# Split activations and split weights laid out in changing orders in SBUF

## The chip, the cores and the metric

The kernel runs on one core of a Trainium2 chip. The metric is the device time of one execution in microseconds (us). TensorE (PE) multiplies: a weight load (LDWEIGHTS, PEld in the profile) brings 128 columns of a stationary operand into the array, and a matmul streams a moving operand past it and adds into a bank of PSUM. VectorE (DVE), ScalarE (ACT) and GpSimd (POOL) work element by element; SyncE (SP) issues most of the DMAs from HBM. SBUF holds 128 partitions; what is called the layout here is the order of elements within a partition.

## The reference

Two layers over 256 tokens of 2048 channels, all in float32: a state-space mixer (S5) with a gated output, then attention over a sliding window of 128; each is followed by a SwiGLU feed-forward of width 5632. Before each part and at the end stands a norm.

```python
def reference(x, ...):
    h = x
    for i in range(DEPTH):
        hn = rmsnorm(h, norm_mix[i])
        if i % N_MIXERS == 0:
            mix = s5_mixer(hn, ...)            # out = gl[..., :dm] * sigmoid(gl[..., dm:]), gl = gelu(y) @ w_glu
        else:
            mix = sliding_window_attention(hn, ...)   # hn @ w_qkv + b_qkv, softmax with sinks, o @ w_o
        h = h + mix
        hn = rmsnorm(h, norm_ffn[i])
        h = h + swiglu(hn, ...)                # (silu(x @ w_gate) * (x @ w_up)) @ w_down
    return rmsnorm(h, norm_final)
```

## The kernel before

**Products in three passes.** The matmuls read float32 in a form called float32r here, with less precision than float32. So every weight and every activation is split into a high part (the value rounded to float32r) and a low part (what is left), and each product is three matmuls: high x high, high x low and low x high. These are lines 734, 735 and 736 in `products`. The activations are the stationary operand (128 channels on partitions, 128 tokens as columns), the weights the moving one (128 channels, 512 columns), and the sum of 128 tokens x 512 outputs is one PSUM bank, `acc`.

**Weights.** `Weights` cuts all weight matrices into 332 pieces of 512 x 512 in the order in which they are used: 32 for the gate of S5, 88 + 44 for the first feed-forward, 20 for queries, keys and values, 16 for the attention's output, 88 + 44 for the second. A piece is loaded by one DMA of SP (`load`, L106) into a tile `raw` as [128 partitions, 4 blocks `a`, 512]. `split` then has ACT write the high part (L120) and DVE the low part (L121) into a tile `w` of [128, 2 parts, 4 blocks, 512], 16 KB a partition. There are three places for `w`, used in turns (`place`): two in the pool `wq`, one in the pool `wp`; the piece with a number that is a multiple of three goes to `wp`. `next` hands out piece i, has pieces up to i + 2 split and up to i + 4 loaded.

**Activations.** Four kinds of tiles hold split activations, each of [128 channels, 2 parts, 4 blocks, 256 tokens] and 8 KB a partition: `gt` (the gelu outputs of S5), `hT` (the hidden values of the feed-forward) and `oT` (the attention's outputs), all from `turned_tile` in the pool `pp`; and `xT` (the normed rows, turned), from `normed_tile` in the pool `wp`. PE turns blocks of 128 x 128 into PSUM, ACT writes the high part from there, and DVE the low part: L777 and L778 for `xT`, L857 and L858 for `hT`, L687 and L688 for `gt`, L1008 and L1009 for `oT`.

**Order.** `linear` makes 128 tokens x 512 outputs twice: for each piece it goes over four blocks and two halves of the tokens, so a piece is 4 x 2 x 3 = 24 matmuls (`piece`). Between pieces it takes small jobs from two lists, `left` and `slots`: turning the activations that an earlier product made, loading `h`, or a part of the attention. A framework puts the instructions of each engine in order by its own scheduling, sets the semaphores, and hands out the places of the tiles (`bufs` is the number of places of a tag); `pin` and `keep_in_program_order` hold an instruction in its written place.

**Before the products.** `s5` computes S5 itself: DVE steps through the states (L500, L503, L505), and PE does small products in plain float32. In it lie two lines that the prediction reads: L259 in `lay`, which turns 128 x 128 blocks of `Bn` (in which the columns taken lie 16 elements apart) and of `Cn` (in which they lie next to each other); and L594 in `lags`, where the moving operand is `k[:, :, g2]`, runs of 16 elements with the next 16 left out. ACT and DVE write (L453, L451) and read (L655) the state tiles `V` with a step of 64 elements between neighbours; L600 writes runs of 16 elements.

**Pools in SBUF.** In the order in which they are opened: `cp` (`ident`, 128 elements; `gcol`, 48; `ylast`, 512), `pp` (four tiles of 8 KB and two `raw` of 8 KB), `wq` (two `w`), and after S5 `wp` (`h`, two tiles of 8 KB; `ssq`, two of 8 elements; one `w`; `junk` and `act`; four `xT`; small ones).

Of the kernel before, what the change touches and what calls it, by code (L numbers as in the profile page):

```python
# [17 lines left out]
P = 128  # L18
D = 2048
# [27 lines left out]
def bc(ap, axis, n):  # L47
    """`ap` with a repeated axis of n put in."""
    v = ap.unsqueeze(axis)
    shape = list(v.shape)  # L50
    shape[axis] = n
    return v.to_broadcast(shape)
# [3 lines left out]
def kernel(  # L56
# [25 lines left out]
    # parts of activations, channels on partitions: [channel, high/low, 128 channels, token]  # L82
    def turned_tile(name):
        return pp.tile([P, 2, 4, T], F32R, tag="b8", name=nm(name))

    def normed_tile(name):
        return wp.tile([P, 2, 4, T], F32R, tag="xt", name=nm(name), bufs=4)

# [1 line left out]
    class Weights:  # L90
# [18 lines left out]
        def place(self, i):  # L109
            """in turns, but for the first the third place isn't there yet"""  # L110
            pool, n = (wp, 1) if i % 3 == 0 and i > 0 else (wq, 2)
            return pool.tile([P, 2, 4, 512], F32R, tag="w", name=nm("w"), bufs=n)

        def split(self, upto, keep=lambda ins: ins):
            while len(self.hl) < min(upto, len(self.src)):
                i = len(self.hl)
                self.load(i + 1)
                w = self.place(i)
                hi, lo = w[:, 0], w[:, 1]
                keep(S.activation(hi, self.raw[i], AF.Copy))  # L120
                keep(V.tensor_tensor(lo, self.raw[i], hi.bitcast(F32), op=ALU.subtract))  # L121
                self.hl.append((hi, lo))
# [40 lines left out]
    # the last heads come while the first two chunks of the outputs have what the others give  # L163
# [12 lines left out]
    # work that an earlier product left for the tensor engine, done between a later one's pieces  # L176
    left = []
    # the same, a list for each of the next pieces
    slots = []

# [1 line left out]
    def s5():  # L182
        st = ExitStack()
        with st:
# [8 lines left out]
            def pin(ins):  # L193
                """in this place among its engine's work"""
# [8 lines left out]
            # the states; until then, room for what does not stay  # L203
# [4 lines left out]
            # loads  # L208
# [34 lines left out]
            # masks: row (j, g2, c) belongs to g2 = 0 / 1 ; sign of the re / im half  # L243
# [11 lines left out]
            def lay(nat):  # L255
                """banks of [(re/im, state), channel, group]"""
# [5 lines left out]
            def laid(pts, name, sign):  # L262
                """[(re/im, state), group, channel], times a sign per partition"""
# [5 lines left out]
            # the norm of x: rows' sums of squares  # L269
# [11 lines left out]
            # the norm's weights go into B (and D)  # L281
# [5 lines left out]
            # the other norms' weights, channels on partitions  # L287
# [4 lines left out]
            # parameters, [group, state]  # L292
# [42 lines left out]
            # powers of lambda: [group, power - 1, re/im, state]  # L335
# [5 lines left out]
            def cmul(o, a, b, n):  # L341
                """o = a * b, complex, [G, n, 2, NS]; b has one power"""
# [11 lines left out]
            # q = (lambda - 1) / a ; XQ[j] = lambda^(3-j) q  # L354
# [19 lines left out]
            # the same with the state (twice) on partitions: [(2, state), power, re/im, group]  # L374
# [21 lines left out]
            # tokens: U[(j, g2, c), pair, g2' (other group's rows zero), chunk]; a quarter of the pairs  # L396
            # is eight of each half of the channels
# [24 lines left out]
            def at(pair):  # L422
                """quarter and place in it"""
# [5 lines left out]
            # X[j] = lambda^(3-j) q B ; what each chunk adds to the states  # L429
            X = []  # L430

            def turned_x(q, b):
# [3 lines left out]
                xt = lp.tile([P, 4, P], F32, tag="xt", name=nm("xt"), bufs=5)  # L436
# [18 lines left out]
            def split_groups(ap, t):  # L455
                """the quarter's groups, of an AP with groups second"""
# [30 lines left out]
            # states at the chunks' ends, for half of the quarters; what a chunk adds is there already  # L487
            reached = [0, 0]

            def step(hf, parts=1):  # L490
                """in as many parts as it takes to hide an operation's latency"""
# [19 lines left out]
            # lambda^4 in [(g2, state), product, re/im, quarter, half, pair]  # L511
# [45 lines left out]
            # D of a chunk's channels, on the diagonal: [(lag 0, g2, c), pair, c']  # L557
# [16 lines left out]
            # K[(lag, g2, c), pair, c'], lag 3 - j, and  # L574
            # M[(j, g2, c), pair, j', c'] = K of lag j' - j
# [5 lines left out]
            def kernels(t):  # L581
# [5 lines left out]
                k = lp.tile([P, 16, 2, GC], F32, tag="xt", name=nm("k"), bufs=5)  # L587
# [15 lines left out]
            # what a chunk's own tokens give its outputs  # L603
# [22 lines left out]
            # T[(re/im, state), group, j', c'] = what a chunk's first state gives its outputs  # L626
# [12 lines left out]
            # the states laid out as each chunk's first state  # L639
# [28 lines left out]
            # the states' room goes to the first weights  # L668
# [4 lines left out]
            # outputs, gelu, channels onto partitions  # L673
# [42 lines left out]
    def rms_scale(pool, ssq, shape, keep=lambda ins: ins, between=lambda: None):  # L716
        """1 / sqrt(ssq / D + eps)"""
# [14 lines left out]
    def products(acc, xq, w, a, t, first, last):  # L732
        x_ = xq[:, :, a, t * P : (t + 1) * P]
        PE.matmul(acc, x_[:, 0], w[0][:, a], start=first, stop=False)  # L734
# [3 lines left out]
    def piece(acc, xq, first, last):  # L738
        """the next piece of the weights with 512 channels"""
# [359 lines left out]
```

## Time and profile before

| | |
|---|---|
| median of the runs | 2145.8 us (2 runs, 2145.72 to 2145.88) |
| span of the profiled execution | 2144.7 us |
| PE busy in it | 2044.8 us |
| DVE, ACT, POOL busy | 1177.0, 907.1, 99.8 us |
| matmuls L734 + L735 + L736 | 3 x (1568 xT + 704 hT + 256 gt + 128 oT) = 7968 |
| read from HBM | 356.91 MB, 167 GB/s over the span |

The profile is one execution, recorded by the hardware. PE's busy time counts matmuls that overlap (a matmul with 512 columns lasts some 390 ns from its first read to its last write, and the next one begins before it has ended), so what a matmul costs is the distance from its start to the next start. A row of the timeline reads: start in us, duration in us, engine, line, operation, tiles written <- tiles read, and in brackets how long the engine had stood idle and what released it. A row of groups ends with the busy time of all, the mean ns of one, and the idle time before them with what ended it. A row on one line's instructions gives minimum / median / maximum of the duration in ns, and the first and the last start. In the windows, the first number is the length of the window; the busy times of PE, PEld, DVE, ACT and POOL follow, each with its count, then the granted clock, the DMA share and GB/s.

### The profile page before, as it was taken

The page shows a single profiled execution, that of the slowest core. Times are in us where ns is not written, and L with a number is a line of the kernel's source. Part 1 is how long each engine was busy: PE and PEld are TensorE (multiplying, and loading weights), DVE is VectorE, ACT ScalarE, POOL GpSimd, SP SyncE. Part 2 cuts the span into 40 slices and gives each one's busy share as a digit, 9 for nine tenths or more (in the row PEclk, how much of TensorE's full clock was granted, in tenths as well). Part 3 has the DMA queues.
Part 4 walks back from the last instruction along what each step waited for, and adds up shares of the span by engine and source line. Part 5 has one row for each costly group of instructions (what it writes and reads, how often), then busy time and mean ns, then how long its engine had stood idle before and what let it go on. Part 6 is the DMA issues. An engine that isn't in the chain of part 4 may idle for free.

```text
span 2144.7 us, 23467 instructions
## 1 busy us (share of the span) xinstructions
PE 2044.8 (95%) x9724; PEld 1674.3 (78%) x9724; DVE 1177.0 (55%) x1432; ACT 907.1 (42%) x957; POOL 99.8 (5%) x73
## 2 busy tenths in 40 slices
PE   5854999999999999999999999999999999999998
PEld 4754888888888888888888777888888888888886
DVE  8997554544444454445455776544444445444445
ACT  4737444433333333333344554443333333333333
POOL 6450100000000000000000000000000000000000
PEclk8767999999999999999999999999999999999999
DMA  4000666565555555565555433555555555655554
GB/s 120 1 21 21 226 196 193 181 194 178 190 186 193 180 193 192 180 194 180 196 177 185 143 118 119 177 184 189 178 195 189 184 190 184 196 182 191 187 187 156
DMA packets 182731, 360.53 MB, mean 168 GB/s; under 512 B 10592, under 2 KB 10656, under 8 KB 182240
## 3 DMA queue, kind: packets, MB, share of 16 engines
q1 hardware_dynamic: 181376, 355.54, 51.0%
q10 hardware_dynamic: 816, 2.16, 0.3%
q0 software_dynamic: 432, 1.33, 0.3%
q8 instruction: 76, 1.25, 0.2%
q14 instruction: 31, 0.25, 0.0%
HBM read 356.91 MB, written 2.10 MB: 167 GB/s over the span
## 4 chain that ended last, share of the span: by engine, by line
PE 88%; DVE 9%; ACT 1%; DMA 1%; issue 1%; DVEq 0%; ACTq 0%
PE acc L734 28%; PE acc L736 28%; PE acc L735 28%; DVE sc L500 2%; DVE V L503 1%; DVE V L505 1%; PE tr L855 1%; DVE X L469 1%; DVE w L121 1%; PE py L698 1%; PE tr L774 0%; DMA raw<-in_s_w_glu_dram 0%; PE po L1002 0%; ACT w L120 0%; PE tr L991 0%
## 5 line engine op out<-in xcount | busy, mean ns | idle before, releaser
L121 DVE TENSOR_TENSOR w<-raw,w 128x2048 fp32r<-128x2048 f32 x332 | 761.0, 2292 | 859.4 <-ACT w L120 859.4
L120 ACT ACTIVATE w<-raw 128x2048 fp32r<-128x2048 f32 x332 | 636.2, 1916 | 987.9 <-PE acc L736 843.9
L734 PE MATMUL acc<-w,xT 128*128 128x512 f32 x1568 | 618.7, 395 | 0.0
L735 PE MATMUL acc<-w,xT 128*128 128x512 f32 x1568 | 617.0, 393 | 0.0
L736 PE MATMUL acc<-w,xT 128*128 128x512 f32 x1568 | 617.0, 393 | 0.0
L736 PEld LDWEIGHTS acc<-w,xT 128*128 128x128 f32 x1568 | 294.0, 187 | 69.5 <-issue 1.0
L734 PEld LDWEIGHTS acc<-w,xT 128*128 128x128 f32 x1568 | 294.0, 188 | 68.9 <-issue 1.3
L735 PEld LDWEIGHTS acc<-w,xT 128*128 128x128 f32 x1568 | 294.0, 188 | 67.8 <-issue 0.5
L734 PE MATMUL acc<-w,hT 128*128 128x512 f32 x704 | 277.3, 394 | 0.0
L736 PE MATMUL acc<-w,hT 128*128 128x512 f32 x704 | 274.8, 391 | 0.0
L735 PE MATMUL acc<-w,hT 128*128 128x512 f32 x704 | 274.1, 390 | 0.0
L736 PEld LDWEIGHTS acc<-w,hT 128*128 128x128 f32 x704 | 132.2, 188 | 29.4
L734 PEld LDWEIGHTS acc<-w,hT 128*128 128x128 f32 x704 | 132.3, 188 | 28.2 <-ACT hT L857 1.2
L735 PEld LDWEIGHTS acc<-w,hT 128*128 128x128 f32 x704 | 132.3, 188 | 28.1
L735 PE MATMUL acc<-w,gt 128*128 128x512 f32 x256 | 99.9, 390 | 0.9 <-DVE w L121 0.9
L734 PE MATMUL acc<-w,gt 128*128 128x512 f32 x256 | 100.7, 394 | 0.0
L736 PE MATMUL acc<-w,gt 128*128 128x512 f32 x256 | 100.1, 391 | 0.0
L698 PE MATMUL py<-T,S 128*64 128x64 f32 x256 | 16.2, 241 | 51.5 <-DVE V L505 51.5
L882 DVE TENSOR_TENSOR h<-h,acc 128x512 f32<-128x512 f32 x64 | 43.6, 687 | 26.5 <-PE acc L736 26.5
L735 PEld LDWEIGHTS acc<-w,gt 128*128 128x128 f32 x256 | 48.1, 188 | 11.7 <-DVE w L121 1.5
L868 ACT ACTIVATE act<-acc,ry 128x512 f32<-128x512 f32 x44 | 30.2, 687 | 62.3 <-PE acc L736 62.1
L736 PEld LDWEIGHTS acc<-w,gt 128*128 128x128 f32 x256 | 48.1, 188 | 10.7
(241 smaller groups left out, 1471.0 us busy)
## 6 DMA issues: line engine op xcount, KB each, us to landing
raw<-in_ffn_w_gate_dram SPq DMA_DIRECT2D x88, 1024.0 KB, 5.2
raw<-in_ffn_w_up_dram SPq DMA_DIRECT2D x88, 1024.0 KB, 5.2
raw<-in_ffn_w_down_dram SPq DMA_DIRECT2D x88, 1024.0 KB, 5.1
raw<-in_s_w_glu_dram SPq DMA_DIRECT2D x32, 1024.0 KB, 5.3
raw<-in_attn_w_qkv_dram SPq DMA_DIRECT2D x20, 1024.0 KB, 5.1
raw<-in_attn_w_o_dram SPq DMA_DIRECT2D x16, 1024.0 KB, 5.0
xk<-in_x_dram SPq DMA_DIRECT2D x8, 256.0 KB, 7.2
h<-in_x_dram SPq DMA_DIRECT2D x2, 1024.0 KB, 7.6
```

Source lines behind the costliest of these rows:

```text
L120: keep(S.activation(hi, self.raw[i], AF.Copy))
L121: keep(V.tensor_tensor(lo, self.raw[i], hi.bitcast(F32), op=ALU.subtract))
L469: ins = eng.tensor_tensor(o[:, :, j].rearrange("p (h a) (g c) -> p h a g c", g=2, h=2), bc(split_groups(XQT[:, j, ri], t).rearrange("p h ( ...
L500: V.tensor_tensor(t_, ws[..., part], bc(Vt[hf][:, k - 1, :, part], 1, 2), op=ALU.mult)
L503: V.tensor_tensor(v, v, t_[:, 0], op=ALU.add)
L505: V.tensor_tensor(v, v, t_[:, 1, ::-1], op=ALU.add)
L698: PE.matmul(py[m][h * NK : (h + 1) * NK, i, g2], St[t][:, a, g2], Tt[q][:, 2 * pq + g2].rearrange("p a b -> p (a b)"), start=False, stop=i ...
L734: PE.matmul(acc, x_[:, 0], w[0][:, a], start=first, stop=False)
L735: PE.matmul(acc, x_[:, 0], w[1][:, a], start=False, stop=False)
L736: PE.matmul(acc, x_[:, 1], w[0][:, a], start=False, stop=last)
L868: S.activation(s, pg[t], AF.Silu, scale=r[0][:, t : t + 1])
L882: V.tensor_tensor(hc, hc, acc[t], op=ALU.add)
```

## The change

No operation is added or removed. Four things change.

- **Order of split activations.** A tile is now 2048 elements a partition, seen in one of four orders in turns: parts, blocks, tokens ("r a n", as before); blocks, tokens, parts ("a n r", neighbouring tokens 2 elements apart); parts, tokens, blocks ("r n a", 4 apart); tokens, blocks, parts ("n a r", 8 apart). The four `xT` tiles of a norm take the four orders one each; the tiles of `turned_tile` go through them backwards.
- **Order of split weights.** A piece is now four blocks, and in each block the two parts lie in turns of e elements: 16, 32, 64, 128, or whole rows of 512. In one piece of six (e = -512) the rows are read backwards by PE, and the product writes the bank of sums backwards.
- **Where tiles begin.** `cp` has a pad of 48 elements more, and `ssq` is 32 elements instead of 8.
- **Fewer places.** `xt` (and `k`) of S5 5 to 4, `junk` 2 to 1, `bias` 2 to 1, `pT` 3 to 2.

Comments and docstrings go as well.

```diff
+    ORDERS = ("r a n", "a n r", "r n a", "n a r")
+    TOGETHER = (512, -512, 16, 32, 64, 128)
+    turn = [0, 0]
+
+    def part(t, kind):
+        return t.rearrange(f"p ({ORDERS[kind]}) -> p r a n", r=2, a=4)
+
     def turned_tile(name):
-        return pp.tile([P, 2, 4, T], F32R, tag="b8", name=nm(name))
+        turn[0] += 1
+        return part(pp.tile([P, 8 * T], F32R, tag="b8", name=nm(name)), turn[0] * 3 % 4)
 
     def normed_tile(name):
-        return wp.tile([P, 2, 4, T], F32R, tag="xt", name=nm(name), bufs=4)
+        turn[1] += 1
+        t = wp.tile([P, 8 * T], F32R, tag="xt", name=nm(name), bufs=4)
+        return part(t, (turn[1] - 1) % 4)
...
             pool, n = (wp, 1) if i % 3 == 0 and i > 0 else (wq, 2)
-            return pool.tile([P, 2, 4, 512], F32R, tag="w", name=nm("w"), bufs=n)
+            return pool.tile([P, 4096], F32R, tag="w", name=nm("w"), bufs=n)
 
         def split(self, upto, keep=lambda ins: ins):
             while len(self.hl) < min(upto, len(self.src)):
                 i = len(self.hl)
                 self.load(i + 1)
                 w = self.place(i)
+                e = TOGETHER[(i // 3 + 2 * i) % 6]
+                n = abs(e)
+                w = w.rearrange("p (a g r e) -> p r a g e", a=4, r=2, e=n)
+                raw = self.raw[i].rearrange("p a (g e) -> p a g e", e=n)
                 hi, lo = w[:, 0], w[:, 1]
-                keep(S.activation(hi, self.raw[i], AF.Copy))
-                keep(V.tensor_tensor(lo, self.raw[i], hi.bitcast(F32), op=ALU.subtract))
-                self.hl.append((hi, lo))
+                keep(S.activation(hi, raw, AF.Copy))
+                keep(V.tensor_tensor(lo, raw, hi.bitcast(F32), op=ALU.subtract))
+                if e < 0:
+                    hi, lo = hi[..., ::-1], lo[..., ::-1]
+                self.hl.append((hi, lo, e < 0))
...
+    cp.tile([P, 48], F32, name="pad")
...
-                xt = lp.tile([P, 4, P], F32, tag="xt", name=nm("xt"), bufs=5)
+                xt = lp.tile([P, 4, P], F32, tag="xt", name=nm("xt"), bufs=4)
...
     def products(acc, xq, w, a, t, first, last):
         x_ = xq[:, :, a, t * P : (t + 1) * P]
+        if w[2]:
+            acc = acc[:, ::-1]
         PE.matmul(acc, x_[:, 0], w[0][:, a], start=first, stop=False)
...
-            self.ssq = wp.tile([P, 2, NCH], F32, tag="ssq", name=nm("ssq"), bufs=2)
+            ssq = wp.tile([P, 32], F32, tag="ssq", name=nm("ssq"), bufs=2)
+            self.ssq = ssq[:, : 2 * NCH].rearrange("p (t n) -> p t n", t=2)
...
-            junk = wp.tile([P, 512], F32, tag="junk", name=nm("junk"), bufs=2)
+            junk = wp.tile([P, 512], F32, tag="junk", name=nm("junk"), bufs=1)
...
-                b = ap.tile([P, 512], F32, tag="bias", name=nm("bias"), bufs=2)
+                b = ap.tile([P, 512], F32, tag="bias", name=nm("bias"), bufs=1)
...
-                        pT = ap.tile([P, 3, P], F32, tag="pT", name=nm("pT"), bufs=3)
+                        pT = ap.tile([P, 3, P], F32, tag="pT", name=nm("pT"), bufs=2)
```

More of the change, by code (lines that the diff above doesn't have):

```diff
@@ L586, in kernels @@
                               start=True, stop=True)
[L587 removed]
+                k = lp.tile([P, 16, 2, GC], F32, tag="xt", name=nm("k"), bufs=4)
                 pin(S.copy(k, pk))
```

## The prediction

> **What bounds the kernel.** I read the page first: the span, the busy shares, the slices, the clock and the chain.
>
> ```profile
> span 2144.7 us, 23467 instructions
> PE 2044.8 (95%) x9724; PEld 1674.3 (78%) x9724; DVE 1177.0 (55%) x1432; ACT 907.1 (42%) x957; POOL 99.8 (5%) x73
> ...
> PE   5854999999999999999999999999999999999998
> ...
> PEclk8767999999999999999999999999999999999999
> ...
> PE 88%; DVE 9%; ACT 1%; DMA 1%; issue 1%; DVEq 0%; ACTq 0%
> PE acc L734 28%; PE acc L736 28%; PE acc L735 28%; DVE sc L500 2%; DVE V L503 1%; DVE V L505 1%; PE tr L855 1%; DVE X L469 1%; DVE w L121 1%; PE py L698 1%; PE tr L774 0%; DMA raw<-in_s_w_glu_dram 0%; PE po L1002 0%; ACT w L120 0%; PE tr L991 0%
> ```
>
> The chain is 88% TensorE, 83% of it in the three matmuls L734 to L736. From the fifth slice on PE is at nine tenths and the granted clock too. Next come the windows, cut at the first long product; columns are PE, PEld, DVE, ACT, POOL busy, then the clock.
>
> ```profile
> 0.00:238.00 238.00, 150.97 (x1149) 134.23 (x1149) 205.07 (x593) 134.28 (x231) 98.15 (x70) 0.74 0.21 61
> 238.00:2136.00 1898.00, 1893.70 (x8575) 1540.03 (x8575) 968.84 (x831) 771.14 (x723) 1.62 (x3) 1.00 0.56 181
> ```
>
> In the last 1898 us PE is busy for 1893.70 at clock 1.00, so no wait is left there to remove. That stretch is 332 pieces of weights with 24 matmuls each, 7968 in all, and the time between two matmul starts (the pitch) is the kernel. In the first 238 us DVE is busy for 205 and the clock is 0.74: another regime, which the change hardly touches.
>
> The pitch is read best from ACT, which begins a split 0.2 us after a piece has freed its place; the distance of two starts is one piece. The first four lines are pieces with xT as stationary operand, the last four with hT.
>
> ```profile
> 956.78 1.92 ACT L120 ACTIVATE w<-raw 128x2048 fp32r<-128x2048 f32 x1 [2.97 <-PE acc L736]
> 962.38 1.91 ACT L120 ACTIVATE w<-raw 128x2048 fp32r<-128x2048 f32 x1 [3.68 <-PE acc L736]
> 967.98 1.92 ACT L120 ACTIVATE w<-raw 128x2048 fp32r<-128x2048 f32 x1 [3.69 <-PE acc L736]
> 973.44 1.93 ACT L120 ACTIVATE w<-raw 128x2048 fp32r<-128x2048 f32 x1 [3.54 <-PE acc L736]
> ...
> 1001.66 1.92 ACT L120 ACTIVATE w<-raw 128x2048 fp32r<-128x2048 f32 x1 [3.52 <-PE acc L736]
> 1007.17 1.93 ACT L120 ACTIVATE w<-raw 128x2048 fp32r<-128x2048 f32 x1 [3.59 <-DVE h L882]
> 1012.66 1.92 ACT L120 ACTIVATE w<-raw 128x2048 fp32r<-128x2048 f32 x1 [3.56 <-PE acc L736]
> 1018.10 1.92 ACT L120 ACTIVATE w<-raw 128x2048 fp32r<-128x2048 f32 x1 [3.52 <-PE acc L736]
> ```
>
> With xT, two pieces take 5.60 us (233.3 ns a matmul) and the third 5.46 (227.5). With hT the three take 5.51, 5.49 and 5.44. The slow ones are those whose operands begin 64 bytes apart, modulo 128. Added up in the order of use, cp holds 512 + 192 + 2048 = 2752 bytes, 64 more than a multiple of 128, so hT, gt, oT and two of the three places of w begin at 64; in wp two ssq of 32 bytes bring w and xT to 0. (That cp itself begins at a multiple of 128 is assumed.) xT against w in wq: 64 apart, 5.60; against w in wp: 0 apart, 5.46; hT against w in wp: 64 apart, 5.51, else 5.49 and 5.44. So the load and the stream do meet in SBUF, and it costs 0.14 us a piece, 5.8 ns a matmul.
>
> ```profile
> L734 PE MATMUL acc<-w,xT 128*128 128x512 f32 x1568 | 618.7, 395 | 0.0
> ...
> L734 PEld LDWEIGHTS acc<-w,xT 128*128 128x128 f32 x1568 | 294.0, 188 | 68.9 <-issue 1.3
> ```
>
> The load of the next stationary operand takes 188 ns beside a matmul and fits inside the pitch: 39 to 45 ns are spare. The 1568 matmuls a line make 196 pieces with xT; 136 are left for the others. Mean pitch: (196 x (2 x 5.60 + 5.46) / 3 + 136 x 5.48) / 332 = 5.52 us a piece, 230 ns.
>
> **The change, part by part.** No matmul, split, load or DMA is added or taken away. What moves is how operands lie.
>
> *Stationary operands.* xT, hT, gt and oT cycle through four orders with tokens 1, 2, 4 and 8 elements apart (4 to 32 bytes), a quarter each. Only one stationary operand of before is not contiguous: Bn at L259, 16 elements (64 bytes) apart; Cn on the same line is contiguous.
>
> ```profile
> L259 PEld LDWEIGHTS ps<-ident,Bn x16: 187/226/227, 11.5 to 14.6; 128*128 128x128 f32 x16
> L259 PE MATMUL ps<-ident,Bn x16: 417/418/480, 11.5 to 14.8; 128*128 128x128 f32 x16
> L259 PEld LDWEIGHTS ps<-ident,Cn x16: 185/231/232, 24.9 to 28.0; 128*128 128x128 f32 x16
> L259 PE MATMUL ps<-ident,Cn x16: 420/421/477, 24.9 to 28.2; 128*128 128x128 f32 x16
> ```
>
> First of its row the load takes 187 ns (strided) against 185, in the queue 226 against 231, and sixteen take 3.1 us both times. Those loads ran at half clock or unrecorded clock and with ordinary float32, so this is no full proof, but they fetch one element from each of 128 places in no more time. I take 0 for the load. From above: ACT reads V 256 bytes apart in 1068 ns where a contiguous copy of the same size takes 587 (rows below), 1.82 times; a load 1.82 times 188 is 342 ns, which no longer fits in 230. From below: 0, since a load gets no shorter than contiguous. I choose by the first row because it is the same engine and port.
>
> *Moving operands.* w has high and low parts in turns of 16, 32, 64 or 128 elements, or in whole rows of 512, or rows read backwards with the sum written backwards (a sixth each). Of the turns the trace has the smallest: L594 streams k in runs of 16 with 16 left out, L596 is contiguous and follows it directly.
>
> ```profile
> 116.36 2.06 PE L594 MATMUL ko<-k,own 128*128 128x256 f32 x4
> 118.34 1.22 PE L596 MATMUL ko<-dd,ident 32*128 32x128 f32 x4
> 119.49 2.08 PE L594 MATMUL ko<-k,own 128*128 128x256 f32 x4
> ```
>
> Four matmuls of 256 columns take 118.34 - 116.36 = 1.98 us, four of 128 contiguous ones 1.15: per column 1.93 against 2.25 ns, so runs cost nothing; I take 0. Nothing in the trace runs backwards. Bounds: 0, since each line and bank is touched as often as forwards, and a pitch twice as long. I take 0, nearer to the runs.
>
> *Where tiles begin.* A pad of 192 bytes and ssq of 128 instead of 32 bring all these operands to 0 modulo 128. If every piece went at the aligned rate, 131 pieces with xT would gain 0.14 us (18.3) and 45 with hT, gt or oT 0.07 (3.2): 21.5 us. But parts in turns begin at 64 again and spread tokens meet other lines than before. Bounds: 0 and -21.5; I take half, -11.
>
> *The splits and the writes of the spread tiles.*
>
> ```profile
> L121 DVE TENSOR_TENSOR w<-raw,w 128x2048 fp32r<-128x2048 f32 x332 | 761.0, 2292 | 859.4 <-ACT w L120 859.4
> L120 ACT ACTIVATE w<-raw 128x2048 fp32r<-128x2048 f32 x332 | 636.2, 1916 | 987.9 <-PE acc L736 843.9 <-DVE h L882 89.7 <-DMA raw<-in_s_w_glu_dram 19.5
> ...
> L858 DVE TENSOR_TENSOR hT<-tr,hT 128x512 fp32r<-128x512 f32 x44 | 28.2, 682 | 0.0
> ...
> L453 ACT COPY V<-pv 64x256 f32<-64x256 f32 x44 | 26.2, 599 | 4.0 <-PE pv L443 3.4
> ...
> L857 ACT CAST hT<-tr 128x512 fp32r<-128x512 f32 x44 | 23.2, 579 | 0.0
> ...
> L655 ACT COPY S<-V 64x512 f32<-64x512 f32 x16 | 17.1, 1068 | 29.0 <-DVE V L505 28.9
> ...
> L451 DVE COPY V<-pv 64x256 f32<-64x256 f32 x20 | 12.0, 598 | 3.2 <-ACT V L453 2.7
> ...
> L600 ACT COPY M<-ko 32x256 f32<-32x256 f32 x40 | 14.6, 364 | 7.6 <-PE ko L596 7.1
> ...
> L1009 DVE TENSOR_TENSOR oT<-po,oT 128x256 fp32r<-128x256 f32 x16 | 6.6, 415 | 12.2 <-ACT oT L1008 12.2
> ...
> L1008 ACT CAST oT<-po 128x256 fp32r<-128x256 f32 x16 | 5.9, 368 | 22.8 <-PE po L1004 22.8
> ...
> L588 ACT COPY k<-pk 128x512 f32<-128x512 f32 x4 | 2.3, 587 | 12.2 <-PE pk L585 12.2
> ```
>
> The split writes runs of 64 bytes or more. L600 writes just that (64-byte runs, 364 ns against 368 for a contiguous 256), so L120 and L121 stay; even at twice 1.92 and 2.29 us they would end within two pieces of 5.5. Tokens 16 or 32 bytes apart, half of the tiles, may cost what L453 does (256 bytes apart): 599 - 368 = 231 ns for 256 elements on ACT, and 598 - 415 = 183 on DVE. For hT that is 0.46 us on 579 and 0.37 on 682. This hides behind pieces of 5.5 us, except where the next matmul asks for hT at once:
>
> ```profile
> PEld acc L734 <- ACT hT L857: 1.2, 4, 0.4
> ```
>
> Four such waits, each up to two writes of 0.46 longer: at most 3.7, half of it taken: +2. The same at the end of S5, where 16 casts to gt (half of them spread, 0.23 each) stand shortly before the first product: 0 to 3.7, +2 taken.
>
> *Fewer buffers.* xt 5 to 4, pT 3 to 2, junk 2 to 1: a reader of the place handed out next stands earlier on PE (or the writer is ACT itself, in order), so the writer waits for nothing new; 0. Without that cover pT would wait for a PE matmul four times in a group, under 1 us each. bias 2 to 1:
>
> ```profile
> L1026 ACT ACTIVATE bias<-bias 128x512 f32<-128x512 f32 x4 | 2.5, 632 | 17.4 <-DMA bias<-in_attn_b_qkv_dram 17.4
> ```
>
> ACT stands in this multiplication until POOL's DMA lands, and the next split stands behind it on ACT and PE behind that. Now the DMA is issued one chunk later, after the DVE reads of the chunk before; with four pieces (22 us) until q reads it, and a wait of 17.4 / 4 = 4.4 us each as now, it comes at another moment and takes no more time; 0. If ACT stood there 11 us, a piece would come late.
>
> *Sum.* 2144.7 (this execution's span) - 11 + 2 + 2 = 2137.7. The runs' median of 2145.8 is 1.1 above the span: **2139 us**, -0.3%.
>
> **Rivals.**
>
> *Loads collide in proportion to their lines* (slower, the other side). Being 64 bytes apart costs 5.8 ns for a load of contiguous tokens. If every load paid that by the places it touches, 1, 2, 4 and 4 times as many: 5.8, 11.7, 23.3, 23.3, a mean of 16 ns on the aligned 227.5. 7968 x 16 = 128, less the 21.5: +106, **2252 us**. For it: the 5.60 and 5.46 above. Against it: Bn. It decides from a mean pitch of 235 on (2% is 43 us or 5.4 ns).
>
> *The load outlasts the matmul.* Half of the matmuls at 342 ns: 3984 x 112 = 446, **2592 us**. For it: the rows of ACT and DVE (L655, L453, L451). Against it: L259, and that 39 ns are spare. The Trainium skill (Advanced Engine Details and Errata, SBUF Cachelines) says that full speed needs at least two hits on a 16-byte line; by that rule 4-byte tokens 16 and 32 bytes apart are slow and 8 apart are not. Here ACT's L453 agrees with it and TensorE's L259 does not.
>
> *Backwards costs double.* 55 pieces, 1328 matmuls, 230 ns more each: +305, **2451 us**. Nothing in the trace speaks for or against it. The Trainium skill (PSUM — Partial Sum Buffer, Specifications) says that any non-contiguous pattern in PSUM slows matmuls; whether a step of -1 counts as one it does not say, and no run here shows it yet.
>
> *Turns take the two streams apart.* If parts in turns kept load and stream from meeting at all, another step of 5.8 ns under 227.5 could go: pitch 221.7, 8.3 under the mean, 7968 x 8.3 = 66: **2080 us**. For it: that where operands lie matters at all. Against it: no row goes under 5.44 us a piece.
>
> **How the numbers follow.** "No change", everything between 2103 and 2189, has 0.58: the engine that decides shows no cost in the two rows nearest to the change. Its own range is 2117 to 2160 (the full alignment gain, or none with the writes at their ends and a few us of meeting). Proportional collision has 0.18, the long load 0.08, backwards 0.06, together 0.32 slower by over 2% (about what a measurement of this kernel can tell from no change). Faster by over 2% has 0.10. The range 2070 to 2290 takes in no change, the proportional case (2252, or 2274 without the alignment gain) and most of the faster one: 0.58 + 0.18 + 0.06 = 0.82.
>
> **What would show it.** Mean LDWEIGHTS of L734 to L736 still 188 ns, and pieces of equal length whatever the order of the tokens, prove the first step; pieces of two lengths in step with xT's four orders prove a collision or a long load, and the load's mean tells which (188 or about 340). Backwards shows as every sixth piece long, in MATMUL durations beyond 395. Alignment shows as 5.46 where 5.60 stood. Spread writes show in L778 and L858 and in waits of PE for hT. Wrong it is if one of the six ways of w or of the four of the tokens alone is slow: the mean of any one counts by a sixth or a quarter, and a quarter at +24 ns is already 2%.

## The result, and the profile after

| | before | after |
|---|---|---|
| median of the runs, us | 2145.8 | 2205.93 (2 runs, 2205.89 to 2205.97) |
| ratio, 95% interval | | 1.0279 [1.0259, 1.0298] |
| span of the profiled execution, us | 2144.7 | 2204.2 |

The changed kernel is slower, by 60 us or 2.8%. First the page of the changed kernel: the span, the busy times, and groups of the first of the three product lines (L756 to L758 now) and of the writes to `hT` (L880 and L881). A group ends with busy time and mean ns of one, then the idle time before them.

```profile
span 2204.2 us, 23485 instructions
...
PE 2104.8 (95%) x9724; PEld 1907.6 (87%) x9724; DVE 1197.7 (54%) x1432; ACT 928.6 (42%) x957; POOL 98.2 (4%) x73
...
L756 PE MATMUL acc<-w,xT 128*128 128x512 f32 x1568 | 630.8, 402 | 0.0
...
L756 PEld LDWEIGHTS acc<-w,xT 128*128 128x128 f32 x1568 | 400.0, 255 | 34.0 <-issue 1.3
...
L756 PEld LDWEIGHTS acc<-w,hT 128*128 128x128 f32 x704 | 183.4, 261 | 14.9 <-ACT hT L880 1.4
...
L881 DVE TENSOR_TENSOR hT<-tr,hT 128x512 fp32r<-128x512 f32 x44 | 38.5, 918 | 0.0
...
L880 ACT CAST hT<-tr 128x512 fp32r<-128x512 f32 x44 | 36.1, 904 | 0.0
```

The number of matmuls and loads is the same, but the mean load went from 188 to 255 ns and PEld's busy time from 1674 to 1908 us. PE still waits for nothing: the idle time before L756 with `xT` stays at 0.0. The windows, cut at the same first edge as before, show where the time came in (length; then busy times of PE, PEld, DVE, ACT, POOL; granted clock, DMA share, GB/s).

```profile
0.00:238.00 238.00, 149.80 (x1140) 135.85 (x1141) 206.59 (x593) 135.28 (x230) 96.00 (x69) 0.74 0.20 60
238.00:2196.00 1958.00, 1955.04 (x8585) 1771.74 (x8584) 988.29 (x832) 791.64 (x724) 2.17 (x4) 1.00 0.54 176
```

The stretch of the products was 1898 us long and is 1958 at the same clock of 1.00: 60 us, all of the difference, or 7.5 ns on each of 7968 matmuls. So the pitch grew. Which pieces grew is read, as before, from the starts of ACT's split: the distance of two rows is one piece.

```profile
986.32 1.92 ACT L136 ACTIVATE w<-raw 128x2048 fp32r<-128x2048 f32 x1 [3.67 <-PE acc L758]
991.97 1.91 ACT L136 ACTIVATE w<-raw 128x2048 fp32r<-128x2048 f32 x1 [3.73 <-PE acc L758]
...
1044.38 1.92 ACT L136 ACTIVATE w<-raw 128x2048 fp32r<-128x2048 f32 x1 [3.79 <-PE acc L758]
1050.24 1.91 ACT L136 ACTIVATE w<-raw 128x2048 fp32r<-128x2048 f32 x1 [3.95 <-PE acc L758]
1055.94 1.92 ACT L136 ACTIVATE w<-raw 128x2048 fp32r<-128x2048 f32 x1 [3.79 <-PE acc L758]
1061.42 1.92 ACT L136 ACTIVATE w<-raw 128x2048 fp32r<-128x2048 f32 x1 [3.55 <-PE acc L758]
1067.34 1.92 ACT L136 ACTIVATE w<-raw 128x2048 fp32r<-128x2048 f32 x1 [4.01 <-PE acc L758]
1073.04 1.92 ACT L136 ACTIVATE w<-raw 128x2048 fp32r<-128x2048 f32 x1 [3.78 <-PE acc L758]
1078.64 1.91 ACT L136 ACTIVATE w<-raw 128x2048 fp32r<-128x2048 f32 x1 [3.68 <-PE acc L758]
```

In order of time: tokens 4 apart with whole rows 5.65 us; then, from 1044.38 on, 8 apart with whole rows 5.86, 2 apart with turns of 16 5.70, 1 apart with turns of 64 5.48, 8 apart backwards 5.92, 1 apart with turns of 32 5.70, 2 apart with turns of 128 5.60. The lengths follow both orders. The mean pitch of each pair, from the starts of L756 to L758 over the whole trace without the gaps between pieces, in ns:

| tokens apart | 512 | 512 backwards | 16 | 32 | 64 | 128 | mean load |
|---|---|---|---|---|---|---|---|
| 1 | 228.0 | 233.4 | 241.8 | 237.3 | 227.9 | 228.1 | 188 |
| 2 | 233.7 | 234.0 | 237.9 | 237.9 | 233.0 | 233.1 | 195 |
| 4 | 235.1 | 233.3 | 239.9 | 241.1 | 235.0 | 235.2 | 310 |
| 8 | 244.5 | 246.9 | 238.7 | 243.4 | 244.3 | 244.4 | 327 |

The mean of these is 237, of before 230.2. The load can be seen piece by piece: the rows of L756 within a single piece each, tokens 1, 2, 4 and 8 apart (minimum, median, maximum of the duration in ns; first and last start).

```profile
L756 PEld LDWEIGHTS acc<-w,xT x8: 187/188/194, 1090.5 to 1095.3; 128*128 128x128 f32 x8
...
L756 PEld LDWEIGHTS acc<-w,xT x8: 193/193/308, 981.0 to 985.9; 128*128 128x128 f32 x8
...
L756 PEld LDWEIGHTS acc<-w,xT x9: 308/310/320, 985.9 to 991.5; 128*128 128x128 f32 x9
...
L756 PEld LDWEIGHTS acc<-w,xT x9: 192/330/333, 1084.0 to 1089.8; 128*128 128x128 f32 x9
```

8 bytes between tokens leave the load almost as it was, 16 and 32 bytes make it 1.65 and 1.76 times as long. (The odd 308 and 192 belong to a neighbouring piece.)

### The profile page after: what moved, and what is told of

It is laid out like the page before. It is cut to its first block, busy times and chain, and to the rows that moved or that the text cites. A ratio compares the mean times of both kernels' runs of the same rounds, so it can differ in the third digit from the quotient of the medians.

```text
span 2204.2 us, 23485 instructions
## 1 busy us (share of the span) xinstructions
PE 2104.8 (95%) x9724; PEld 1907.6 (87%) x9724; DVE 1197.7 (54%) x1432; ACT 928.6 (42%) x957; POOL 98.2 (4%) x73
## 4 chain that ended last, share of the span: by engine, by line
PE 87%; DVE 9%; ACT 2%; issue 1%; DMA 0%; DVEq 0%; SPq 0%; ACTq 0%; POOLq 0%
PE acc L756 28%; PE acc L758 28%; PE acc L757 28%; DVE sc L520 2%; DVE V L525 1%; DVE V L523 1%; PE tr L878 1%; DVE X L489 1%; ACT sc L998 1%; DVE w L137 1%; PE tr L796 0%; PE po L1025 0%; PE tr L1014 0%; PE py L718 0%; DVE sc L986 0%
## 5 line engine op out<-in xcount | busy, mean ns | idle before, releaser
L756 PE MATMUL acc<-w,xT 128*128 128x512 f32 x1568 | 630.8, 402 | 0.0
L758 PE MATMUL acc<-w,xT 128*128 128x512 f32 x1568 | 628.4, 401 | 0.0
L757 PE MATMUL acc<-w,xT 128*128 128x512 f32 x1568 | 627.4, 400 | 0.0
L756 PEld LDWEIGHTS acc<-w,xT 128*128 128x128 f32 x1568 | 400.0, 255 | 34.0 <-issue 1.3
L757 PEld LDWEIGHTS acc<-w,xT 128*128 128x128 f32 x1568 | 400.5, 255 | 33.1 <-issue 0.5
L758 PEld LDWEIGHTS acc<-w,xT 128*128 128x128 f32 x1568 | 399.4, 255 | 34.2 <-issue 1.0
L756 PE MATMUL acc<-w,hT 128*128 128x512 f32 x704 | 283.9, 403 | 0.4 <-ACT hT L880 0.3
L757 PE MATMUL acc<-w,hT 128*128 128x512 f32 x704 | 281.3, 400 | 0.0
L758 PE MATMUL acc<-w,hT 128*128 128x512 f32 x704 | 281.1, 400 | 0.0
L756 PEld LDWEIGHTS acc<-w,hT 128*128 128x128 f32 x704 | 183.4, 261 | 14.9 <-ACT hT L880 1.4
L757 PEld LDWEIGHTS acc<-w,hT 128*128 128x128 f32 x704 | 183.8, 261 | 13.4
L758 PEld LDWEIGHTS acc<-w,hT 128*128 128x128 f32 x704 | 183.2, 260 | 13.7
L757 PE MATMUL acc<-w,gt 128*128 128x512 f32 x256 | 102.4, 400 | 0.9 <-DVE w L137 0.9
L756 PE MATMUL acc<-w,gt 128*128 128x512 f32 x256 | 102.9, 403 | 0.0
L758 PE MATMUL acc<-w,gt 128*128 128x512 f32 x256 | 102.4, 400 | 0.0
L757 PEld LDWEIGHTS acc<-w,gt 128*128 128x128 f32 x256 | 65.4, 255 | 6.6 <-DVE w L137 1.4
L756 PEld LDWEIGHTS acc<-w,gt 128*128 128x128 f32 x256 | 65.2, 255 | 5.4
L758 PEld LDWEIGHTS acc<-w,gt 128*128 128x128 f32 x256 | 65.2, 255 | 5.4
```

Of the source, the lines that this page charges most:

```text
L757: PE.matmul(acc, x_[:, 0], w[1][:, a], start=False, stop=False)
L758: PE.matmul(acc, x_[:, 1], w[0][:, a], start=False, stop=last)
```

## The experiments

The theory after the result: the load of tokens 16 and 32 bytes apart is long enough to set the pitch by itself, and the turns and the backwards reading cost something of their own. The rival: load and stream meet in SBUF more or less often, by where both lie, and neither is long by itself. The first four kernels ran on one chip and shared its runs of the kernel before (median 2146.47 us).

**Tokens alone.** Of the changed kernel, all weights in whole rows, forwards; tokens, places and pads as in the change.

```diff
-    TOGETHER = (512, -512, 16, 32, 64, 128)
+    TOGETHER = (512,) * 6
```

> All weights lie in whole rows of 512 read forwards; the four orders of the tokens, the pad, ssq and the fewer places stay as in the changed kernel. Theory A (spread tokens lengthen the weight load, which then sets or disturbs the pitch): in the trace of the changed kernel the pitch with such weights is 228.0, 233.7, 235.1 and 244.5 ns for tokens 1, 2, 4 and 8 apart, a mean of 235.3 against 230.2 before, so some 40 us over before and a few for the writes: 2186 to 2192 us. Rival B (the weights' turns and backward rows carry the loss): near 2125 to 2135 us.

Measured: 2189.76 us, ratio 1.0202 [1.0187, 1.0217]. Pitch 227.8, 233.3, 235.0, 244.5 with tokens 1, 2, 4, 8 apart, loads 188, 193, 310, 329 ns. That is inside what theory A gave, 2186 to 2192.

**Weights alone.** Tokens contiguous, weights as in the change.

```diff
-        return part(pp.tile([P, 8 * T], F32R, tag="b8", name=nm(name)), turn[0] * 3 % 4)
+        return part(pp.tile([P, 8 * T], F32R, tag="b8", name=nm(name)), 0)
...
-        return part(t, (turn[1] - 1) % 4)
+        return part(t, 0)
```

> All tokens lie next to each other; the weights keep their six orders. From the changed kernel's pitches with contiguous tokens (228.0, 233.4, 241.8, 237.3, 227.9, 228.1 ns for whole rows, backwards, turns of 16, 32, 64, 128; mean 232.8 against 230.2 before) theory A and B together give some 20 us over before: 2163 to 2169 us. If A alone were right: 2125 us. If the two parts add up, this run and the one with tokens alone are together as far above the one with neither as the changed kernel is (80 us); if they hide each other the sum is larger than that.

Measured: 2162.04 us, ratio 1.0073 [1.0058, 1.0088]. The timeline of ACT in this kernel:

```profile
1036.02 1.92 ACT L136 ACTIVATE w<-raw 128x2048 fp32r<-128x2048 f32 x1 [3.86 <-PE acc L758]
1041.49 1.91 ACT L136 ACTIVATE w<-raw 128x2048 fp32r<-128x2048 f32 x1 [3.55 <-PE acc L758]
1047.09 1.91 ACT L136 ACTIVATE w<-raw 128x2048 fp32r<-128x2048 f32 x1 [3.69 <-DVE h L905]
1052.79 1.92 ACT L136 ACTIVATE w<-raw 128x2048 fp32r<-128x2048 f32 x1 [3.78 <-PE acc L758]
1058.25 1.92 ACT L136 ACTIVATE w<-raw 128x2048 fp32r<-128x2048 f32 x1 [3.54 <-PE acc L758]
1064.02 1.92 ACT L136 ACTIVATE w<-raw 128x2048 fp32r<-128x2048 f32 x1 [3.86 <-PE acc L758]
```

In order of time: turns of 64 take 5.47 us, backwards 5.60, turns of 32 5.70, turns of 128 5.46, turns of 16 5.77. Over the whole trace the pitches are 227.2 (512), 233.4 (backwards), 240.8 (16), 237.3 (32), 227.7 and 227.8 (64, 128). Mean over those at 226.9 of the next kernel: 5.5 ns, times 7968 = 44 us; 42 were measured. The time lies 1 us under the 2163 to 2169 that were expected, as whole rows and turns of 16, taken at 228.0 and 241.8 ns, came to 227.2 and 240.8.

**Places alone.** Both edits together: contiguous tokens, whole rows; what is left of the change are the pads and the fewer places.

> Neither order changes: tokens contiguous, weights in whole rows forwards, but with the pad, the larger ssq and the fewer places. Theory C (only being 64 bytes apart modulo 128 cost time before): every piece at 227 to 228 ns, 7968 x 2.4 ns less than before and nothing for the places: 2125 to 2129 us, a ratio of 0.991. Rival D (the fewer places cost time): 2146 us or more, with new waits of PE.

Measured: 2120.06 us, ratio 0.9876 [0.9859, 0.9892]: 26.4 us faster than before, and beyond what was expected. The mean pitch is 226.9 ns, and none of the operands or places is far from it: 226.7 to 227.1 with `xT`, `hT` and `gt`, 226.8 to 228.0 with `oT`.

**Orders alone.** The whole change but for the pad in `cp` and the longer `ssq`.

```diff
-    cp.tile([P, 48], F32, name="pad")
...
-            ssq = wp.tile([P, 32], F32, tag="ssq", name=nm("ssq"), bufs=2)
+            ssq = wp.tile([P, 8], F32, tag="ssq", name=nm("ssq"), bufs=2)
```

> The changed kernel with pad and ssq as before, so that some operands begin 64 bytes apart again. If that distance counts only where both streams are contiguous (1 of 4 orders of tokens, 3 of 6 of the weights, so an eighth of the pairs, at most 3 us): 2206 to 2210 us. If it shifts every pair as it did before: 2220 to 2230 us.

Measured: 2208.47 us, ratio 1.029 [1.0274, 1.0305]. Over the before of its own chip this is +62.0, the whole change +60.1. So the pads that bring 26.4 us to contiguous operands bring 2 to the changed ones, too little to be told from nothing by these times (the two ratios' intervals overlap). The number was as expected, but not for the reason given: without the pads it is not the contiguous pairs alone that take longer. In whole rows, tokens 1 apart go from 228.0 to 230.0 ns and 4 apart from 235.1 to 237.7, while 2 apart go from 233.7 down to 232.8. The four kernels as a sum: tokens cost 69.7 over places alone, weights 42.0, together 111.7; the whole change costs 60.1 + 26.4 = 86.5. Some 25 us overlap, and the table of pairs shows where: a pair takes about the longer of its two pitches, not both surcharges, and 8 apart with turns of 16 (238.7) takes less than either by itself (244.5 and 241.8). Why that is so was not tried.

**All tiles 8 apart.** Of the changed kernel: whole rows, and every tile in the order "n a r".

```diff
-        return part(pp.tile([P, 8 * T], F32R, tag="b8", name=nm(name)), turn[0] * 3 % 4)
+        return part(pp.tile([P, 8 * T], F32R, tag="b8", name=nm(name)), 3)
...
-        return part(t, (turn[1] - 1) % 4)
+        return part(t, 3)
```

> Weights in whole rows, every split activation with tokens 8 elements apart (the fourth order in all tiles): one suspected cost, taken four times. If the price is a matter of each pair of a load and a stream, every pitch is 244.5 ns: 2120 + 7968 x (244.5 - 226.9) = 2260 us, and up to 10 more for the writes. If it came from changing between orders, or from what lies near by, it is less: 2190 or under.

Measured: 2270.9 us, ratio 1.0581 [1.055, 1.0612], pitch 244.7 in every place of `w`. A group of its page:

```profile
L756 PEld LDWEIGHTS acc<-w,xT 128*128 128x128 f32 x1568 | 515.1, 329 | 1.3 <-issue 1.3
```

The idle time before the loads, 68.9 us before the change, is 1.3: the loads leave no gap any more. That alone does not show that the load sets the pitch: where a load lasts 329 ns and the pitch is 244.7, no gap can be left, whatever sets it. The time shows that the price belongs to the pair of a load and a stream and not to changing orders; which of the two is slow is asked in the bench below.

**The pads by themselves.** The kernel before, with only the two pads; the numbers of places as before.

```diff
+    cp.tile([P, 48], F32, name="pad")
...
-            self.ssq = wp.tile([P, 2, NCH], F32, tag="ssq", name=nm("ssq"), bufs=2)
+            ssq = wp.tile([P, 32], F32, tag="ssq", name=nm("ssq"), bufs=2)
+            self.ssq = ssq[:, : 2 * NCH].rearrange("p (t n) -> p t n", t=2)
```

> The kernel before with two edits alone, the pad of 48 elements and ssq of 32 instead of 8, so that all operands of the products begin at the same place modulo 128 bytes; orders and numbers of places as before. Theory C (where they begin is the whole gain): 2119 to 2122 us, as the run with neither order. Rival E (rows of one block's high and low part side by side, or the fewer places, gave part of it): between 2122 and 2146.

Measured: 2120.03 us, ratio 0.9879 [0.9863, 0.9896], against 2120.06 with the fewer places, and the ratios are 0.9879 and 0.9876. So the fewer places cost nothing that these runs can tell (each interval is some 3 us to either side), and the pads are the whole gain. No version tried was faster than these two. Its ACT timeline, where before had 5.60, 5.60, 5.46:

```profile
1061.42 1.92 ACT L120 ACTIVATE w<-raw 128x2048 fp32r<-128x2048 f32 x1 [3.52 <-PE acc L737]
1066.86 1.92 ACT L120 ACTIVATE w<-raw 128x2048 fp32r<-128x2048 f32 x1 [3.52 <-PE acc L737]
1072.30 1.92 ACT L120 ACTIVATE w<-raw 128x2048 fp32r<-128x2048 f32 x1 [3.52 <-PE acc L737]
1077.75 1.92 ACT L120 ACTIVATE w<-raw 128x2048 fp32r<-128x2048 f32 x1 [3.53 <-PE acc L737]
```

5.44 or 5.45 us in all three places of `w`.

**A bench in the kernel.** Three kernels add matmuls to places alone, behind the first feed-forward; the results go nowhere, and their own times mean nothing. All read two tiles of float32r, `xs` (stationary) and `mt` (moving), that begin a multiple of 8 KB apart. The core of it:

```diff
+        def go(name, stat, mov, out=lambda b: b, rows=P, cols=512, n=16):
+            b = bank([P, 512], name)
+            for _ in range(n):
+                pin(PE.matmul(out(b[:rows, :cols]), stat, mov, start=True, stop=True))
...
+        def every(s, q=0):
+            return xt_[:, q : q + 128 * s].rearrange("p (n s) -> p n s", s=s)[:, :, 0]
...
+        for nme, s in (("ldd", 8), ("ldc", 4), ("ldb", 2), ("lda", 1), ("lde", 16)):
+            warm()
+            go(nme, every(s), few, cols=16, n=10)
+        for nme, s in (("lwd", 8), ("lwc", 4), ("lwb", 2), ("lwa", 1), ("lwe", 16)):
+            warm()
+            go(nme, every(s), whole, n=24)
```

The first bench had no `warm` (30 plain matmuls that hold the clock up) in between.

> The kernel with neither order, with 504 matmuls more between the first feed-forward and the attention, whose results go nowhere: loads alone (16 columns streamed, tokens 1, 2, 4, 8, 16 elements apart: lda to lde), the same loads beside 512 contiguous columns (lwb to lwe for 2, 4, 8, 16), streams alone (a load of 32 contiguous columns: sta forwards, stb backwards in both, stc backwards read only, std backwards written only, ste to stg turns of 16, 32, 64), the same streams beside a load of 128 contiguous columns (boa to bog), and both contiguous but beginning 16, 32, 48, 64, 96 and 112 bytes apart (da to df). Theory A1 (a load of tokens 16 bytes or more apart takes twice the time and at 8 apart ends after the stream): lda and ldb 107 ns a matmul, ldc to lde 213 or more, and ldd as long as the 244.5 ns found beside a stream. Rival A2 (the load is hidden, the two only meet): ldd at 213 to 220. Theory B1 (runs of 16 and backward rows are slower streams by themselves): ste 235 to 242 and stb 233, as beside a load. Rival B2 (they only meet the load): ste and stb at 216 to 220 like sta. da to df: 227 at 0, 233 at 64 bytes, others in between. The whole run is some 120 us longer than without.

Measured (2234.72 us, one run): alone, beside matmuls of 16 columns, loads of tokens 1, 2, 4, 8, 16 apart take 112, 118, 233, 238.5 and 217 ns. But the clock fell to 0.50 in the third of these series, so the last ones could have been long for that reason. For 8 apart, theory A1 had expected 244.5 and the rival 213 to 220; 238.5 is neither. Streams beside loads of only 32 columns took 231 (whole), 233 (backwards), 240 (16), 236 (32), 232 (64). The second bench repeats the disputed ones with the clock held up.

> The measurement by itself again, with 30 ordinary matmuls (6.8 us) ahead of each form, since in the first the clock fell to one half during the loads alone. Theory A1 (at full clock a load of tokens 4 or 8 elements apart takes twice as long as a contiguous one and sets the pitch by itself): lda 112, ldb 118, ldc 233, ldd 238 as before, beside a stream 235 and 245. Rival A2 (the 233 and 238 were the half clock): ldc and ldd at 112 to 180, and the loss beside a stream is a meeting of the two. Streams: reading backwards 233 with either load, writing backwards as forwards, turns of 16 at 240 with either load. Beginning apart (da 4 bytes, db 8, dc 16, dd 20, de 32, df 64, dg 128): dc and dg at 227, de and df at 233; the others are not known.

Measured (2400.18 us, one run). The timeline of loads (start, time from the first start to the last end, count), first alone:

```profile
1139.13 2.46 PEld L1102 LDWEIGHTS ldd<-mt,xs 128*128 128x128 f32 x10
1141.49 6.71 PEld L1102 LDWEIGHTS wa<-mt,xs 128*128 128x128 f32 x30
1148.24 2.41 PEld L1102 LDWEIGHTS ldc<-mt,xs 128*128 128x128 f32 x10
1150.56 8.29 PEld L1102 LDWEIGHTS wa<-mt,xs 128*128 128x128 f32 x30
...
1167.11 1.08 PEld L1102 LDWEIGHTS lda<-mt,xs 128*128 128x128 f32 x9
1168.12 6.67 PEld L1102 LDWEIGHTS wa<-mt,xs 128*128 128x128 f32 x30
```

From row to row: 8 apart 2.36 us for ten, 236 ns each; 4 apart 232; contiguous 1.01 for nine, 112. (The distance of neighbouring matmul starts within a series gives 238.4, 233.9 and 111.7, and for 16 apart 216.7.) At full clock, with hardly a stream beside it, a load of tokens 4 or 8 apart takes twice as long, from its start to the next. Now matmuls of 512 columns, where the distance from a series to the 30 `wa` behind it is 24 pitches:

```profile
1183.93 6.03 PE L1102 MATMUL lwd<-mt,xs 128*128 128x512 f32 x24
1189.80 6.97 PE L1102 MATMUL wa<-mt,xs 128*128 128x512 f32 x30
1196.60 5.80 PE L1102 MATMUL lwc<-mt,xs 128*128 128x512 f32 x24
1202.24 6.97 PE L1102 MATMUL wa<-mt,xs 128*128 128x512 f32 x30
1209.05 5.76 PE L1102 MATMUL lwb<-mt,xs 128*128 128x512 f32 x24
1214.65 6.97 PE L1102 MATMUL wa<-mt,xs 128*128 128x512 f32 x30
1221.46 5.60 PE L1102 MATMUL lwa<-mt,xs 128*128 128x512 f32 x24
1226.90 6.97 PE L1102 MATMUL wa<-mt,xs 128*128 128x512 f32 x30
...
1295.98 5.77 PE L1102 MATMUL boc<-mt,xs 128*128 128x512 f32 x24
1301.58 6.99 PE L1102 MATMUL wa<-mt,xs 128*128 128x512 f32 x30
1308.40 5.60 PE L1102 MATMUL bod<-mt,xs 128*128 128x512 f32 x24
1313.84 6.96 PE L1102 MATMUL wa<-mt,xs 128*128 128x512 f32 x30
1320.64 5.92 PE L1102 MATMUL boe<-mt,xs 128*128 128x512 f32 x24
1326.40 7.00 PE L1102 MATMUL wa<-mt,xs 128*128 128x512 f32 x30
```

Tokens 8, 4, 2, 1 apart: 5.87, 5.64, 5.60, 5.44 us, or 244.6, 235, 233.3, 226.7 ns, the pitches of the kernel with tokens alone to about 1 ns. So two tiles that lie at rest, with next to no work on ACT and DVE, show the whole cost of the tokens. Below, with contiguous tokens: read backwards (`boc`) 233.3, the sum written backwards (`bod`) 226.7, turns of 16 (`boe`) 240. Beside loads of 32 columns the turns of 16 take 239.9 and reading backwards 233.3, the same pitch as beside loads of 128: these belong to the moving operand.

**Loads at half clock.** The last bench has 70 thin matmuls first, which bring the clock down, and then the loads alone; behind them, at full clock, contiguous operands that begin some bytes apart.

> The kernel with whole parts and contiguous tokens, and behind the first feed-forward 70 matmuls of 16 columns by a contiguous stationary operand, which should bring the granted clock down to 0.50 (the earlier bench fell there after some 4 us of such matmuls); then twelve each by tokens 1, 8, 2, 4, 16 and again 1 elements apart; their results go nowhere. If the clock hid the stride in the prediction's rows, contiguous loads take about 213 ns at 0.50 where they took 112 at 1.00, 2 apart about as much, and 4 and 8 apart 233 to 238 as at full clock: within 15% of each other. If the clock has nothing to do with it, 1 and 2 apart stay at 112 to 118 and 4, 8 apart at 233 to 238. Then at full clock 24 matmuls of 512 columns each, with the stationary operand's first element 16, 48, 80, 112, 144, 192, 256, 272, 384, 512, 768, 1024, 1040 and 2048 bytes further on than the moving one's, beside 8 KB multiples: if only the place modulo 32 bytes mattered, 48, 80, 112, 144, 272 and 1040 would be fast (226.7 ns) like 16; if the place modulo 256 bytes decides, 16, 256, 272, 512, 768, 1024, 1040 and 2048 are fast and the others take 233.3. Time some 2400 us with the added work; it is of no interest.

Measured (2324.02 us, one run). The loads, then the window around them, whose third number from the end is the granted clock:

```profile
1144.92 2.68 PEld L1102 LDWEIGHTS cla<-mt,xs 128*128 128x128 f32 x12
1147.48 2.96 PEld L1102 LDWEIGHTS cld<-mt,xs 128*128 128x128 f32 x12
1150.34 2.66 PEld L1102 LDWEIGHTS clb<-mt,xs 128*128 128x128 f32 x12
1152.88 2.90 PEld L1102 LDWEIGHTS clc<-mt,xs 128*128 128x128 f32 x12
1155.68 2.70 PEld L1102 LDWEIGHTS cle<-mt,xs 128*128 128x128 f32 x12
...
1145.00:1158.00 13.00, 13.00 (x60) 13.00 (x60) 0.79 (x5) 0.00 (x0) 0.00 (x0) 0.50 0.00 0
```

Tokens 1, 8, 2, 4 apart at clock 0.50: 2.56, 2.86, 2.54, 2.80 us for twelve, or 213, 238, 212, 233 ns; 16 apart 217 by its matmuls' starts. The contiguous load doubles with the halved clock and the spread one stays where it was, so at half clock they look nearly alike (within 12%). The trace of before shows the same of contiguous columns in ordinary float32. `Cn` at L259, at clock 0.50, has matmuls that follow each other after 213 ns; L774 turns contiguous blocks of `h` at clock 1.00, and there it is some 109.

```profile
1101.88 1.02 PEld L774 LDWEIGHTS tr<-ident,h 128*128 128x128 f32 x8
```

Where operands begin, both benches together, bytes between the first elements (8 KB multiples left out) and pitch: 16 and 144, 256, 272, 512, 768, 1024, 1040, 2048 at 226.7; 192 at 228.9; 8 at 230.7; 4, 80, 128 and 384 at 232.0 to 232.9; 20, 32, 48, 64 and 112 at 233.1 to 233.4; 96, in the first bench, at 234.0. 0 or 16 bytes modulo 256 fits the fast ones, but for 144; 128 had been expected at 227. The cause of this pattern stays open. It does fit a difference that the prediction saw and did not explain. By its adding up of the pools, `xT` began 64 bytes further on than the weights in `wq` and took 5.60 us (233.3 ns; 233.3 in the bench too), while `hT` began 64 bytes short of those in `wp`, which is 192 modulo 256, and took only 5.51 (229.8 over the trace; 228.9 in the bench). The 5.49 of `hT` at a distance of 0 it does not explain.

## Why the prediction was wrong

The forecast was 2139 us and no change; 2205.93 came, inside the range of 2070 to 2290, and slower by more than 2%, to which 0.32 had been given. That the range held it was luck: it reached that far up for a collision in proportion (2252), and no such collision was found. Step by step:

- **"I take 0 for the load"** is the step that failed. It rested on L259, where tokens 64 bytes apart loaded as fast as contiguous ones. The text itself said that those loads ran at half or unrecorded clock, and then passed over it. In both rows of L259 the matmuls follow each other after 213 ns, and the contiguous one ran at clock 0.50, where the last bench has 213 for a contiguous load alone and 217 for one 64 bytes apart. At 1.00 it is 112 against 217, and L774 shows 109 in the trace that the prediction read. So the two rows were equal because the contiguous one was slow. With whole weights the tokens cost 69.7 us, the largest term of the change. The long load would explain about half of it: alone, loads 4 and 8 apart take 233.9 and 238.4 ns, 7.0 and 11.5 more than the 226.9 of a contiguous pair, and with a quarter of the matmuls each that is an estimated 37 us. The rest does not follow from the load's length. 2 apart takes 118 ns alone and still 233.3 beside a stream, and 8 apart takes 244.6 there, 6 more than alone. Load and stream meet in these cases too, and how is not known. The Trainium skill (Advanced Engine Details and Errata, SBUF Cachelines) has the rule that the prediction set aside for this row: two hits on a 16-byte line are needed for full speed. The runs agree with it for loads alone at full clock: 8 bytes apart 118 ns, 16 and 32 bytes apart 233.9 and 238.4.
- **"Nothing for the turns"** failed too. L594 and L596 were read in a stretch that ran at clock 0.50 as well (by the windows of before, 116 to 121 us), with plain float32. There the turns did cost nothing: behind the first of each series, matmuls follow after some 425 ns for 256 columns in turns and 215 for 128 contiguous ones, 1.7 ns a column in both. Whether it was the clock or the type that hid the price was not tried. At full clock turns of 16 cost some 14 ns a matmul (240.8 over 226.9) and turns of 32 some 10; 64 and 128 cost under 1.
- **Backwards, 0.** Reading backwards costs 6.6 ns, not the 230 of the bound; writing the sum backwards costs 0. The Trainium skill (PSUM — Partial Sum Buffer, Specifications) says that any non-contiguous pattern there slows matmuls; a step of -1 does not count as one here, at 226.7 with and without it. All weights' orders together cost 42.0 us.
- **Where tiles begin, -11 of -21.5.** That it matters where operands begin was right, and for contiguous ones even the bound of -21.5 was too small: they gain 26.4 us, and the pitch went to 226.9, 5.44 us a piece. But the operands of the change are no longer contiguous, and those gain 2, not 11. The modulus was wrong too: 128 bytes apart is as slow as 64 (232.4 and 233.4), 256 is not.
- **The writes, +2 and +2.** ACT's mean write of `hT` went from 579 to 904 ns and DVE's from 682 to 918; the spread ones (4 and 8 apart) take about 1.15 and 1.11 us, 0.57 and 0.43 more than before, where 0.46 and 0.37 were estimated. The wait of PEld for `hT` went from 1.2 to 1.4 us: hidden. The distances of matmul starts over 270 ns add up to 126 us before and 130 after; 3 of that are more than the ordinary pitch in them, which may hold part of the term. It was not tried apart.
- **Fewer places, 0.** Right, as far as the runs can tell: 2120.06 with them, 2120.03 without. The waits of ACT for `bias`, 17.4 us before, are 11.6.
- **The rivals.** "Proportional collision" gave 2252; the mean pitch passed the 235 that it named, but its mechanism is not this one: its steps of 5.8, 11.7, 23.3, 23.3 ns are 0.9, 6.4, 8.1, 17.6 over 226.9 in the kernel with tokens alone, 4 and 8 apart differ though by its count they meet equally many places, and the load is long with hardly a stream beside it. "The load outlasts the matmul", at 0.08, came nearest in mechanism, and its 342 ns are close to the 310 to 330 that a load now lasts in the trace. What was wrong is to take this duration for the pitch. A contiguous load lasts 188 ns in the trace and yet the next can follow after 112; a spread one lasts 330 and the next follows after 238. So half of the matmuls went not to 342 but to 235 and 244.5, 4 and 8% above the 226.9 of contiguous operands. "Turns take the streams apart" did not happen.

The sum with the measured terms: 2145.8 - 26.4 + 69.7 + 42.0 - 25 for the overlap = 2206. The 25 are no measurement of their own: they are what the four kernels leave over, so the sum closes by construction.

## What to carry to other kernels

Lay the columns of a stationary float32r operand next to each other: beside a stream of 512 columns that took 226.7 ns a matmul here, against 233.3 at 8 bytes apart and 235 to 244.6 at 16 to 64. Keep runs of the moving operand at 64 elements or more. Padding so that both begin a multiple of 256 bytes apart gave 1.2% here. Before a row of the profile is taken as the price of a layout, look at the granted clock of its window: loads 32 bytes apart took twice a contiguous one's time at clock 1.00 (238 against 112 ns) and only an eighth more at 0.50 (238 against 213). And price a pipelined instruction by the distance of starts in a series, not by the duration of one.

## What was not expected of the hardware

Tokens 32 bytes apart load more slowly (238.4 ns) than 64 bytes apart (216.7), alone and beside a stream (244.6 and 235.2). Tokens 8 bytes apart load almost as fast as contiguous ones (118 against 112 ns) and still cost a matmul as much, 233.3, as operands that begin 64 bytes apart. A stream beside a load of 32 columns takes 231.5 ns and beside one of 128 columns 226.7, so a shorter load does not make a faster matmul. And matmuls of 16 columns, which keep PE busy for all of a window, let the clock fall from 1.00 to 0.50 after some 4 us in the first bench and 2.3 in the last.
